# FoX queries, z and both merge gates in seven block products, with the token sums kept to the end

## The chip, the cores and the metric

The kernel runs on one core of one Trainium2 chip. The core has five engines with a queue each: TensorE (PE, matmuls into eight PSUM banks of 128 x 512 float32), VectorE (DVE), ScalarE (ACT), GpSimd (POOL) and SyncE (SP, which here only issues DMAs). Every engine works through its own queue in order and waits on semaphores for the others. The metric is the time of one execution in microseconds of device time. Before the change it was 949.82 us, the median of three runs (949.73 to 950.01).

## The reference

One layer of a hybrid decoder on 512 tokens, with 16 meta tokens ahead of them (L = 528), width 1024, in float32. A forgetting attention (FoX, 8 heads of 128) and an mLSTM (4 heads, keys of 256, values of 512) work on the same normalised input; sigmoid gates merge them, and an output projection and a norm follow.

```python
h = rms_norm(x, g_pre)
z = h @ w_in
(fq, fk, fv, ff, fz, mqk, mv, mi, mf, mo, mz, ga, gb) = jnp.split(z, SPLIT_POINTS, axis=-1)
oa = forgetting_attention(fq, fk, fv, log_sigmoid(ff + b_fox_f))      # softmax(scores + decay) v
ya = (oa * silu(fz)) @ w_a
hb = sigmoid(mo) * mlstm_scan(conv_silu(mq), conv_silu(mk), mv, mi, log_sigmoid(mf))
yb = (rms_norm(hb, g_head) * silu(mz)) @ w_b
merged = sigmoid(ga) * ya + sigmoid(gb) * yb
out = x + rms_norm(merged @ w_o, g_post)
```

## The kernel before

Float32 matmuls are made of three products of a two-part split: each operand is cut into a high part (an ACT copy to float32r) and a low part (a DVE subtraction), and `mm3` issues high x high, high x low, low x high (L149 to L151). The input is kept transposed as `hh` and `hl` (128 x 8 x 528), the sixteen meta tokens once more as the packed tile `hm`. Weights come by SP in raw tiles of 512 KB (`wload`, four buffers), and `wsplit` cuts them (ACT L141, DVE L143).

A projection of 256 columns is a *plain* unit: `proj_t` twice, 2 x 8 x 3 = 48 matmuls of 512 columns. The mLSTM's output gate `mo` and its z gate `mz` go by *seven block products* instead (Strassen's scheme in Winograd's form): `st_narrow` loads one half of the rows into r0 and the other into r1 and makes four splits, a (128 x 512, in the buffers `whs` and `wls`, two of each), b, c and d (128 x 1024); POOL adds two block sums into r0 between a and b (L259, L260), DVE two into r1 between c and d (L265, L266). `st_products` multiplies them with sums of token blocks (t1 to t4, made once by `st_tokens` and held in the pool `mlstm`), 84 matmuls of 256 columns in two PSUM banks; ACT takes three snapshots in passing (L313, L317, L321), and DVE combines the result in PSUM (L324, L325, L327).

The order in the program: the mLSTM head by head (h = 0 to 3: q and k with their convolution, values, output gate, then `value_part` of chunks 3 and 2, mz unit 0, chunks 1 and 0, mz unit 1; the transposes `pht` of the head's output follow in `turn_part`, the product with w_b into `yb` in `wb_part`). In `value_part` the sums of squares go to POOL for a power (`pow`, L797), and DVE multiplies the result into `ht` (L798); `pht` transposes `ht`. Then the pool `mlstm` is closed and `fox` is opened in its place. FoX goes by pairs of heads (p = 0 to 3): `fq_part`, `fk_part`, for even p `fv_part` of four heads, `prob_part` (logits `pl` on PE, a reduction on DVE with the decay row `ab`, exponential on ACT, `pn` on DVE and POOL), `ptr_part` (transposes `pt`, splits `pth` and `ptl`), `fz_part`, `fout_part`. The gate `gb` is applied to `yb` on POOL in odd p. At the end come `ga`, the product with w_a, the merge, and w_o.

Which instruction stands where in an engine's queue is set when the program is built: a scheduler orders the instructions of all engines by the order of the code and by its own estimates of when operands and buffers come free. Buffers of one tag come around in a ring: a tile waits until the tile before it in the same buffer has been read for the last time. The same holds for the eight PSUM banks.

## Time and profile before

| | |
|---|---|
| median of three runs | 949.82 us |
| profiled execution | 950.76 us |
| span of its instructions | 949.0 us |
| mean granted TensorE clock | 0.993 |
| busy PE, DVE, ACT, POOL | 930.5, 572.7, 440.0, 139.4 us |

Times in rows of the profile count from the start of the span. A row of the timeline gives start, duration, engine, line, operation, the tile written and the tiles read; in square brackets stands how long the engine had been idle before and what ended that. Names leave the buffer numbers out.

### The profile page before, as it was taken

The numbers are of one execution on the slowest core, as the hardware profiler recorded it, in microseconds if no ns is written. First come the engines' busy times: TensorE is split into PE (matmuls) and PEld (weight loads), VectorE is DVE, ScalarE is ACT, GpSimd is POOL, SyncE is SP. The second block draws the span as 40 slices with busy tenths as digits, with TensorE's granted clock in tenths as the row PEclk, the third lists the DMA queues.
The fourth block names the chain that finished last, engine by engine and source line by source line (L and its number), as shares of the span: only waits on it lengthen the run. The fifth ranks groups of instructions, "written<-read, shape, count | busy, mean of one in ns | idle before, by whom it ended". The sixth has DMA issues, their size and how long they took to land.

```text
span 949.0 us, 14296 instructions
## 1 busy us (share of the span) xinstructions
PE 930.5 (98%) x5720; PEld 835.3 (88%) x5720; DVE 572.7 (60%) x966; ACT 440.0 (46%) x740; POOL 139.4 (15%) x186
## 2 busy tenths in 40 slices
...
GB/s 227 92 62 87 45 112 87 121 27 90 98 103 100 59 75 90 112 78 89 54 100 173 89 129 79 96 96 118 89 96 95 90 71 85 177 89 95 105 23 90
DMA packets 71469, 90.05 MB, mean 95 GB/s; under 512 B 4965, under 2 KB 56261, under 8 KB 71402
## 3 DMA queue, kind: packets, MB, share of 16 engines
...
## 4 chain that ended last, share of the span: by engine, by line
PE 93%; DVE 4%; ACT 1%; issue 1%; DMA 0%; POOL 0%; DVEq 0%; POOLq 0%; ACTq 0%
PE pyb L150 3%; PE pyb L151 3%; PE pyb L149 3%; PE pv L151 3%; PE pv L149 3%; PE pv L150 3%; PE po L149 3%; PE po L150 3%; PE po L151 3%; PE pz L149 3%; PE pz L151 3%; PE pz L150 3%; PE pqk L149 2%; PE pqk L151 2%; PE pqk L150 2%; PE pfk L149 2%
## 5 line engine op out<-in xcount | busy, mean ns | idle before, releaser
L959 POOL TENSOR_SCALAR pn<-lt,rsum 128x128 f32<-128x128 f32 x32 | 23.2, 725 | 208.5 <-DVE rsum L957 208.5
L151 PE MATMUL pyb<-bh,wb_l 128*128 128x512 f32 x128 | 49.8, 389 | 0.0
L150 PE MATMUL pyb<-bl,wb_h 128*128 128x512 f32 x128 | 49.8, 389 | 0.0
L149 PE MATMUL pyb<-bh,wb_h 128*128 128x512 f32 x128 | 49.8, 389 | 0.0
L150 PE MATMUL pv<-wv_l,hh 128*128 128x512 f32 (+1 forms) x128 | 46.6, 364 | 1.5 <-DVE wv_l L143 1.5
L149 PE MATMUL pv<-wv_h,hh 128*128 128x512 f32 (+1 forms) x128 | 46.4, 362 | 0.0
L151 PE MATMUL pv<-wv_h,hl 128*128 128x512 f32 (+1 forms) x128 | 46.4, 362 | 0.0
L690 DVE SCALAR_TENSOR_TENSOR y<-z,gc,y 128x512 f32<-128x512 f32 (+1 forms) x48 | 35.9, 754 | 2.2 <-ACT y L683 1.5
L149 PE MATMUL pqk<-hh,wq_h 128*128 128x258 f32 x128 | 36.4, 284 | 0.0
L149 PE MATMUL pqk<-hh,wk_h 128*128 128x264 f32 x128 | 36.3, 284 | 0.0
L149 PE MATMUL pfk<-hh,wfk_h 128*128 128x264 f32 x128 | 36.3, 284 | 0.0
L151 PE MATMUL pfk<-hh,wfk_l 128*128 128x264 f32 x128 | 36.3, 284 | 0.0
L150 PE MATMUL pfk<-hl,wfk_h 128*128 128x264 f32 x128 | 36.3, 283 | 0.0
L151 PE MATMUL pqk<-hh,wk_l 128*128 128x264 f32 x128 | 36.3, 283 | 0.0
L150 PE MATMUL pqk<-hl,wk_h 128*128 128x264 f32 x128 | 36.2, 283 | 0.0
L151 PE MATMUL pqk<-hh,wq_l 128*128 128x258 f32 x128 | 36.0, 282 | 0.0
L150 PE MATMUL pqk<-hl,wq_h 128*128 128x258 f32 x128 | 36.0, 282 | 0.0
L150 PE MATMUL pout<-wo_l,mh 128*128 128x256 f32 (+1 forms) x96 | 30.6, 318 | 0.0
L151 PE MATMUL pout<-wo_h,ml 128*128 128x256 f32 (+1 forms) x96 | 30.6, 318 | 0.0
L149 PE MATMUL pout<-wo_h,mh 128*128 128x256 f32 (+1 forms) x96 | 30.6, 318 | 0.0
L956 ACT ACTIVATE lt<-lt,mn 128x144 f32<-128x144 f32 (+3 forms) x32 | 18.3, 573 | 24.7 <-DVE mn L951 24.7
L150 PEld LDWEIGHTS pv<-wv_l,hh 128*128 128x128 f32 x128 | 24.1, 189 | 5.5 <-DVE wv_l L143 1.7
...
## 6 DMA issues: line engine op xcount, KB each, us to landing
...
```

The costliest lines, as they stand in the source:

```text
L149: T.matmul(ps, ah, bh, start=start, stop=False, **kw)
L150: T.matmul(ps, ah, bl, start=False, stop=False, **kw)
L151: T.matmul(ps, al, bh, start=False, stop=stop, **kw)
L690: V.scalar_tensor_tensor(y[:, t0:L], z[:, m, t0 + j:L + j], gc[:, j * 16 + mi:j * 16 + mi + 1], y[:, t0:L], ALU.mult, ALU.add)
L956: S.activation(lt[:, 0:kn], lt[:, 0:kn], AF.Exp, bias=mn[:, li:li + 1], scale=-1.0, accum_out=rsum)
L959: G.tensor_scalar(pn[:, o:o + P].rearrange("p (g t) -> p g t", g=4), lt[:, 0:32].unsqueeze(1).to_broadcast([P, 4, 32]), rsum, None, ALU.mult)
```

## The change

Sixteen units change from plain to seven block products: `fq`, `fz`, `gb` and `ga`, four each, by a new helper `st_unit`, which `mz_part` uses as well. For this the token sums t1 to t4 must live to the end; their pool is renamed and never closed, and room is found for it: `whs` and `wls` have one buffer instead of two, the decay rows `ab` one instead of two, `hm` lies in the pad of `hh` (112 partitions in place of 128), the decay table `ac` is packed, the z gate is kept in `yb`, and FoX's output replaces it there. So `yb` times sigmoid(`gb`) goes to DRAM (`d_yb`, from POOL's queue), three of the four sigmoid(`ga`) too (`d_sa`, from ACT's queue), and both come back by SP in the last stage. The order of FoX is new: `ga` 0 and `gb` 0 are done beside the last w_b product, `gb` 1 and `gb` 3 at the end of even p, `gb` 2 and `ga` 1 in odd p, `ga` 2 and `ga` 3 at the end; the four products with w_a then follow each other.

```diff
-BYTES = {"w": 8192, "y": 2304, "vm": 2560, "ptm": 2048, "ab0": 5632, "ab1": 5632, "whs": 2048, "wls": 2048,
-         **{f"qk{i}{x}": 4608 for i in range(2) for x in "hl"}, **{f"v{x}": 8704 for x in "hl"},
-         **{f"big_{x}": 8704 for x in "hl"}}
+BYTES = {"w": 8192, "y": 2304, "vm": 2560, "ptm": 2048, "sg": 4160, "ab": 5632, "whs": 2048, "wls": 2048,
+         **{f"qk1{x}": 4608 for x in "hl"}, **{f"v{x}": 8704 for x in "hl"}, **{f"big_{x}": 8192 for x in "hl"}}
...
+    hhm = cp.tile([P, KC, LP], F32R, name="hh")
+    hh, hm = hhm[:, :, 0:L], hhm[:, :, L:LP]
...
-    c1 = ctx.enter_context(ExitStack())
-    mw = c1.enter_context(tc.tile_pool(name="mlstm", bufs=1))
+    mw = ctx.enter_context(tc.tile_pool(name="sums", bufs=1))
...
-        o = {"a11": split(r0[:, :, a], f"{name}a", ("whs", "wls"), mw, 2)}
+        o = {"a11": split(r0[:, :, a], f"{name}a", ("whs", "wls"), mw, 1)}
         G.tensor_tensor(r0[:, :, a], r0[:, :, a], r0[:, :, b], ALU.add)
         G.tensor_tensor(r0[:, :, b], r0[:, :, b], r1[:, :, b], ALU.add)
...
+    def st_unit(c0, name, room):
+        ps = banks(f"p{name}", 2)
+        st_products(st_narrow(c0, f"w{name}"), [(ps[0], ps[1], room.rearrange("p a (b n) -> p (a b) n", b=2), None)])
+        return ps
     def mz_part(h, u):
         g = sb([P, 2, SEQ], F32, ("qk1h", "qk1l")[u], f"gz{h}{u}")
-        ps = banks(f"pz{h}{u}", 2)
-        snap = g.rearrange("p a (b n) -> p (a b) n", b=2)
-        st_products(st_narrow(C_MZ + h * MV + u * 256, f"wz{h}{u}"), [(ps[0], ps[1], snap, None)])
+        ps = st_unit(C_MZ + h * MV + u * 256, f"z{h}{u}", g)
         for m in range(2):
             S.activation(g[:, m, :], ps[m], AF.Sigmoid)
         for m in range(2):
...
-        w = wchunk(win, 0, KC, C_FQ + p * 256, 256, f"wfq{p}")
-        ps = banks(f"pfq{p}", 2)
-        for m in range(2):
-            proj_t(ps[m], w, m)
+        ps = st_unit(C_FQ + p * 256, f"fq{p}", sb([P, 2, SEQ], F32, "w", f"fqs{p}"))
         s = -(FD ** -0.5)
...
     def fz_part(p):
-        w = wchunk(win, 0, KC, C_FZ + p * 256, 256, f"wfz{p}")
-        ps = banks(f"pfz{p}", 2)
-        for m in range(2):
-            proj_t(ps[m], w, m)
-        sz = sb([P, 2, SEQ], F32, "sz", f"fsz{p}", gp)
+        sz = yb[:, 2 * p:2 * p + 2, :]
+        ps = st_unit(C_FZ + p * 256, f"fz{p}", sz)
         for m in range(2):
             S.activation(sz[:, m, :], ps[m], AF.Sigmoid)
             V.tensor_tensor(sz[:, m, :], ps[m], sz[:, m, :], ALU.mult)
-        return sz
-    def gb_part(u):
-        w = wchunk(win, 0, KC, C_GB + u * 256, 256, f"wgb{u}")
-        ps = banks(f"pgb{u}", 2)
-        for m in range(2):
-            proj_t(ps[m], w, m)
-        sg = sb([P, 2, SEQ], F32, "sgb", f"sgb{u}", gp)
+    def gate_part(c0, u, name):
+        sg = sb([P, 2, SEQ], F32, "sg", f"s{name}{u}", gp)
+        ps = st_unit(c0 + u * 256, f"{name}{u}", sg)
         for m in range(2):
             S.activation(sg[:, m, :], ps[m], AF.Sigmoid)
-        G.tensor_tensor(yb[:, 2 * u:2 * u + 2, :], yb[:, 2 * u:2 * u + 2, :], sg, ALU.mult)
+        return sg
+    def gb_part(u):
+        sg = gate_part(C_GB, u, "gb")
+        y = yb[:, 2 * u:2 * u + 2, :]
+        G.tensor_tensor(y, y, sg, ALU.mult)
+        nc.gpsimd.dma_start(d_yb[u], y)
+    def ga_part(u):
+        nc.scalar.dma_start(d_sa[u], gate_part(C_GA, u, "ga"))
 
     def prob_part(p, m, q, k):
 
         h = 2 * p + m
         qh, ql = q
         kh, kl = k
-        ab = sb([P, NA], F32, ("ab0", "ab1")[m], f"ab{h}", gp)
+        ab = sb([P, NA], F32, "ab", f"ab{h}", gp)
         nc.sync.dma_start(ab, d_na[h:h + 1, :].to_broadcast([P, NA]))
         pn = sb([P, NPACK], F32, "w", f"pn{h}")
...
+        V.tensor_tensor(yb[:, h, :], ps, yb[:, h, :], ALU.mult)
...
+    gp = ctx.enter_context(tc.tile_pool(name="fox", bufs=1))
+    d_yb = [dram.tile([P, 2, SEQ], F32, name=f"d_yb{u}") for u in range(4)]
+    d_sa = [dram.tile([P, 2, SEQ], F32, name=f"d_sa{u}") for u in range(3)]
     q = fq_part(0)
-    c1.close()
-    gp = ctx.enter_context(tc.tile_pool(name="fox", bufs=1))
-    oss = line(gp, "oss", NCH * 3).rearrange("p (b i) -> p b i", i=3)
-    go = gp.tile([P, FH, SEQ], F32, tag="go", name="go")
     k = fk_part(0)
+    ga_part(0)
     wb_part(MH - 1, bt)
+    gb_part(0)
     for p in range(FH // 2):
         if p:
             q = fq_part(p)
-            fout_part(*tail)
+            if p % 2 == 0:
+                fout_part(*tail)
             k = fk_part(p)
         pn0 = prob_part(p, 0, q, k)
         if p % 2 == 0:
             v = fv_part(p)
-            pt0 = ptr_part(p, 0, pn0)
-            pn1 = prob_part(p, 1, q, k)
-            sz = fz_part(p)
-            fout_part(p, 0, pt0, v, sz)
-            pt1 = ptr_part(p, 1, pn1)
         else:
-            sz = fz_part(p)
-            pt0 = ptr_part(p, 0, pn0)
-            pn1 = prob_part(p, 1, q, k)
-            gb_part(p - 1)
-            fout_part(p, 0, pt0, v, sz)
-            pt1 = ptr_part(p, 1, pn1)
-            gb_part(p)
-        tail = (p, 1, pt1, v, sz)
+            fz_part(p)
+        pt0 = ptr_part(p, 0, pn0)
+        pn1 = prob_part(p, 1, q, k)
+        if p % 2 == 0:
+            fz_part(p)
+        elif p == 1:
+            gb_part(2)
+        else:
+            ga_part(1)
+        fout_part(p, 0, pt0, v)
+        pt1 = ptr_part(p, 1, pn1)
+        tail = (p, 1, pt1, v)
+        if p % 2 == 0:
+            gb_part(p + 1)
+            fout_part(*tail)
+    ga_part(2)
+    gs = [gsplit(p, (sb([P, 2, SEQ], F32R, f"qk{p}h", f"gh{p}"), sb([P, 2, SEQ], F32R, f"qk{p}l", f"gl{p}")))
+          for p in range(2)]
+    gs.append(gsplit(2, pair("w", "g2")))
     fout_part(*tail)
-    gs0 = gsplit(0, ("vh", "vl"))
-    sa2 = sb([P, 2, 2, SEQ], F32, "w", "sa")
-    sa0 = ga_part(0, sa2)
...
+    def fetch(tag, name, src):
+        t = sb([P, 2, SEQ], F32, tag, name, mw)
+        nc.sync.dma_start(t, src)
+        return t
     mh_, ml_ = [], []
-    for u, (t, pool) in enumerate((("qk0{}", wk), ("qk1{}", wk), ("ab{}", gp), ("s{}", gp))):
-        th, tl = (t.format(x) for x in (("01", "01", "01", ("z", "gb"))[u] if u > 1 else "hl"))
-        mh_.append(sb([P, 2, SEQ], F32R, th, f"mh{u}", pool))
-        ml_.append(sb([P, 2, SEQ], F32R, tl, f"ml{u}", pool))
-    gs = (gs0, gs1)
+    xr = []
     for u in range(4):
-        sa = sa0 if u == 0 else sa1 if u == 1 else ga_part(u, sa2)
         w2 = wchunk(wa, 0, KC, u * 256, 256, f"wa{u}")
+        sa = fetch(("t3h", "t1h", "t4h")[u], f"sa{u}", d_sa[u]) if u < 3 else sa3
+        sb_ = fetch(("t3l", "t1l", "t4l", "t2h")[u], f"sy{u}", d_yb[u])
         py = banks(f"pya{u}", 2)
         for m in range(2):
             for k in range(KC):
-                gh, gl = gs[k // 4]
+                gh, gl = gs[k // 2]
                 mm3(py[m], w2[0](k, m * P, m * P + P), w2[1](k, m * P, m * P + P),
-                    gh[:, k % 4, :], gl[:, k % 4, :], k == 0, k == KC - 1)
+                    gh[:, k % 2, :], gl[:, k % 2, :], k == 0, k == KC - 1)
         for m in range(2):
             V.tensor_tensor(sa[:, m, :], py[m], sa[:, m, :], ALU.mult)
-        V.tensor_tensor(sa, sa, yb[:, 2 * u:2 * u + 2, :], ALU.add)
-        S.activation(mh_[u], sa, AF.Copy)
-        V.tensor_tensor(ml_[u], sa, f(mh_[u]), ALU.subtract)
+        V.tensor_tensor(sa, sa, sb_, ALU.add)
+        if u < 3:
+            mh, ml = pair(("vl", "big_h", "big_l")[u], f"m{u}")
+        else:
+            mh, ml = sb([P, 2, SEQ], F32R, "ab", "mh3", gp), sb([P, 2, SEQ], F32R, "t2l", "ml3", mw)
+        S.activation(mh, sa, AF.Copy)
+        V.tensor_tensor(ml, sa, f(mh), ALU.subtract)
+        mh_.append(mh)
+        ml_.append(ml)
+        if u < 2:
+            for i in range(2):
+                b = 2 * u + i
+                xr.append(sb([P, DM], F32, (("t3h", "t3l"), ("t1h", "t1l"))[u][i], f"xr{b}", mw))
+                nc.sync.dma_start(xr[b], x2[b * P:(b + 1) * P, :])
```

Three places in the queues (from L187 on, lines of the changed kernel lie up to 19 further on than before: L798 is L806 there, and the multiply L919 is L921). First DVE in mLSTM head 1, from the last sum of squares to the combining of mz unit 0 (`pz_0`, `pz_1`); `wz11a` to `wz11d` are the weight splits of mz unit 1. Before:

```order
L795 TENSOR_SCALAR mss_2541<-mss_2541 128x1
L798 TENSOR_SCALAR ht_2502<-ht_2502,mrs_2544 128x512
L251 TENSOR_TENSOR wz11c_l<-wz_r_2726,wz11c_h 128x1024
L265 TENSOR_TENSOR wz_r_2726<-wz_r_2724,wz_r_2726 128x4x128
L266 TENSOR_TENSOR wz_r_2726<-wz_r_2726 128x4x128
L251 TENSOR_TENSOR wz11d_l<-wz_r_2726,wz11d_h 128x1024
L324 TENSOR_TENSOR pz_1_2549<-gz_2547,pz_1_2549 128x256
L327 TENSOR_TENSOR pz_0_2548<-pz_0_2548,gz_2547 128x512
```

Now:

```order
L803 TENSOR_SCALAR mss_2540<-mss_2540 128x1
L806 TENSOR_SCALAR ht_2501<-ht_2501,mrs_2543 128x512
L251 TENSOR_TENSOR wz11a_l<-wz_r_2723,wz11a_h 128x512
L251 TENSOR_TENSOR wz11b_l<-wz_r_2723,wz11b_h 128x1024
L251 TENSOR_TENSOR wz11c_l<-wz_r_2725,wz11c_h 128x1024
L265 TENSOR_TENSOR wz_r_2725<-wz_r_2723,wz_r_2725 128x4x128
L266 TENSOR_TENSOR wz_r_2725<-wz_r_2725 128x4x128
L251 TENSOR_TENSOR wz11d_l<-wz_r_2725,wz11d_h 128x1024
L324 TENSOR_TENSOR pz_1_2548<-gz_2546,pz_1_2548 128x256
L327 TENSOR_TENSOR pz_0_2547<-pz_0_2547,gz_2546 128x512
```

The narrow split a and split b of unit 1, which were made during the output gate (a stands ahead of `wz10c`, b among the first row sums, further up), now stand between the last multiply into `ht` and split c.

On POOL at the same place the two adds of unit 1 (L259, L260 on `wz_r_2724` before, on `wz_r_2723` now) and the powers. Before:

```order
L259 TENSOR_TENSOR wz_r_2550<-wz_r_2550 128x4x128
L260 TENSOR_TENSOR wz_r_2550<-wz_r_2550,wz_r_2552 128x4x128
L259 TENSOR_TENSOR wz_r_2724<-wz_r_2724 128x4x128
L260 TENSOR_TENSOR wz_r_2724<-wz_r_2724,wz_r_2726 128x4x128
L797 TENSOR_TENSOR mrs_2509<-mss_2506,mhalf 128x1
L797 TENSOR_TENSOR mrs_2544<-mss_2541,mhalf 128x1
```

Now:

```order
L259 TENSOR_TENSOR wz_r_2549<-wz_r_2549 128x4x128
L260 TENSOR_TENSOR wz_r_2549<-wz_r_2549,wz_r_2551 128x4x128
L805 TENSOR_TENSOR mrs_2508<-mss_2505,mhalf 128x1
L805 TENSOR_TENSOR mrs_2543<-mss_2540,mhalf 128x1
L259 TENSOR_TENSOR wz_r_2723<-wz_r_2723 128x4x128
L260 TENSOR_TENSOR wz_r_2723<-wz_r_2723,wz_r_2725 128x4x128
```

The adds have moved behind the two powers of the chunks 3 and 2.

Then DVE in FoX with p = 0, from split b of gate unit 1 on, while PE is in FZ (`pfz` are the two banks of the z gate, `wgb1` the weights of gate unit 1, which PE turns to after `fout` and `pt`). Now:

```order
L251 TENSOR_TENSOR wgb1b_l<-wgb_r_6589,wgb1b_h 128x1024
L965 RECIPROCAL rsum_6414<-rsum_6414 128x1
L969 TENSOR_SCALAR pn_6361<-lt_6402,rsum_6414 128x512
L251 TENSOR_TENSOR wgb1c_l<-wgb_r_6591,wgb1c_h 128x1024
L265 TENSOR_TENSOR wgb_r_6591<-wgb_r_6589,wgb_r_6591 128x4x128
L266 TENSOR_TENSOR wgb_r_6591<-wgb_r_6591 128x4x128
L324 TENSOR_TENSOR pfz_1_6420<-yb,pfz_1_6420 128x256
L325 TENSOR_TENSOR pfz_1_6420<-pfz_1_6420,yb 128x512
L327 TENSOR_TENSOR pfz_0_6419<-pfz_0_6419,yb 128x512
L251 TENSOR_TENSOR wgb1d_l<-wgb_r_6591,wgb1d_h 128x1024
L921 TENSOR_TENSOR yb<-pfz_0_6419,yb 128x512
```

Before, two plain splits of `wfk` stood here among the multiplies that empty `pfz`; now the splits a (further up), b and c of the next block unit and its two adds stand ahead of the combining, and the multiplies (L921) stand behind split d.

More of the change, by code (lines that the diff above doesn't have):

```diff
@@ L185, in proj_wide @@
                 for k in (k0, k0 + 1):
[L186 to L187 removed]
+                    T.matmul(pm[0:MP], hm[:, k, :], w[0](k, 0, 512), start=(k == 0), stop=False)
+                    T.matmul(pm[0:MP], hm[:, k, :], w[1](k, 0, 512), start=False, stop=(k == KC - 1))
     def proj_m(ps, w, n=256):
         for k in range(KC):
[L192 to L193 removed]
+            T.matmul(ps[0:MP], hm[:, k, :], w[0](k, 0, n), start=(k == 0), stop=False)
+            T.matmul(ps[0:MP], hm[:, k, :], w[1](k, 0, n), start=False, stop=(k == KC - 1))
     def v_meta(vm, ps):
[L197 removed]
+        S.activation(vm[0:MP], ps[0:MP], AF.Copy)
         V.tensor_tensor(vm[32:64, :], ps[32:64, :], f(vm[32:64, :]), ALU.subtract)
@@ L418, in v_tiles @@
         G.memset(f(vh[:, :, MV:MV + 2]), 1.0)
[L419 removed]
+        G.memset(f(vm[0:MP, MV:MV + 2]), 0.0)
         G.memset(f(vm[0:32, MV:MV + 2]), 1.0)
[L421 removed]
+        G.memset(f(vm[96:MP, MV:MV + 2]), 1.0)
         return vh, vl, vm
@@ L574, in tile_hybrid_block @@
     for i in range(2):
-        T.transpose(pm2[0:12, i * P:i * P + P], gn[:, NCH, i * 12:i * 12 + 12], ident)
+        T.transpose(pm2[0:12, i * P:i * P + MP], gn[0:MP, NCH, i * 12:i * 12 + 12], ident[0:MP, 0:MP])
     pst = psum1("gct")
@@ L603, in tile_hybrid_block, with acc @@
     V.tensor_tensor(a, gi, bc, ALU.subtract)
-    ac = sb([12, NCH, L], F32, "big_h", "ac")
+    ac = sb([12, NA], F32, "big_h", "ac")
+    def acc(c, k0, k1, rows=12):
+        return ac[0:rows, OFFA[c] + k0:OFFA[c] + k1]
     for c in range(NCH):
         k0, k1 = NM + c * P, NM + (c + 1) * P
-        V.tensor_scalar(ac[:, c, 0:k0], ac[:, c - 1, 0:k0] if c else a[:, 0:k0], bc[:, k0 - 1:k0], None, ALU.add)
-        V.tensor_copy(ac[:, c, k0:k1], a[:, k0:k1])
+        V.tensor_scalar(acc(c, 0, k0), acc(c - 1, 0, k0) if c else a[:, 0:k0], bc[:, k0 - 1:k0], None, ALU.add)
+        V.tensor_copy(acc(c, k0, k1), a[:, k0:k1])
     mp = line(cp, "mp", NCH, 12)
@@ L629, in tile_hybrid_block @@
         k1 = NM + (c + 1) * P
-        G.tensor_scalar(na[:, OFFA[c]:OFFA[c] + k1], ac[0:8, c, 0:k1], -1.0, None, ALU.mult)
+        G.tensor_scalar(na[:, OFFA[c]:OFFA[c] + k1], acc(c, 0, k1, 8), -1.0, None, ALU.mult)
     nc.sync.dma_start(d_na, na)
@@ L636, in columns @@
         for i, (c, j) in enumerate(BLK):
-            T.transpose(pcv[:, i, :], ac[:, c, NM + j * P:NM + (j + 1) * P], ident[0:12, 0:12])
+            T.transpose(pcv[:, i, :], acc(c, NM + j * P, NM + (j + 1) * P), ident[0:12, 0:12])
         for c in range(NCH):
```

63 lines of the change are left out of this document (24 added, 39 removed).

## The prediction

> **What bounds the kernel now.** I read the page first (busy time, slices, chain), then the waits of PE, then the times at which stages start on PE.
>
> ```profile
> span 949.0 us, 14296 instructions
> PE 930.5 (98%) x5720; PEld 835.3 (88%) x5720; DVE 572.7 (60%) x966; ACT 440.0 (46%) x740; POOL 139.4 (15%) x186
> DMA packets 71469, 90.05 MB, mean 95 GB/s; under 512 B 4965, under 2 KB 56261, under 8 KB 71402
> ...
> PE 93%; DVE 4%; ACT 1%; issue 1%; DMA 0%; POOL 0%; DVEq 0%; POOLq 0%; ACTq 0%
> ```
>
> PE is busy 98% of the span and 93% of the chain that ended last, so the kernel lasts as long as its matmuls are issued without a gap. In PE's waits, what stands behind the first 110 us is only this:
>
> ```profile
> PE pl L149 <- DVE fvm L198: 1.3, 2, 0.6
> PE pl L149 <- DVE fsz L919: 1.1, 2, 0.5
> ```
>
> Four waits, 2.4 us in all. So two questions decide the change: how much matmul time it takes away, and whether DVE, ACT and POOL, which get more to do, still deliver before PE arrives. Their average share (60%, 46%, 15%) does not answer the second.
>
> **The gain on PE.** Stage lengths, from the first matmul of a stage to the first of the next:
>
> ```profile
> 810.78 0.39 PE L149 MATMUL pga<-hh,wga_h 128*128 128x512 f32 x1
> ...
> 832.57 0.39 PE L149 MATMUL pya<-gh,wa_h 128*128 128x512 f32 x1
> ```
>
> ```profile
> 488.12 0.28 PE L149 MATMUL pz<-hh,wz30a_h 128*128 128x256 f32 x1
> ...
> 497.85 0.28 PE L777 MATMUL pnb<-vh,wh 128*128 128x258 f32 x1
> ```
>
> Two plain units (96 matmuls of 512 columns) last 21.79 us, 10.90 each. A unit of seven block products (84 of 256 columns) lasts 9.73. Sixteen units change: FQ, FZ, GB, GA, four each. 16 x (10.90 - 9.73) = **18.7 us**. The four waits above disappear too, since the order around them is a new one: 2.4 us. Gain without any new wait: 21.1 us.
>
> **What it adds.** Each unit gains, beside the splits of its weights, a narrow split, two adds on POOL (L259, L260), two adds on DVE (L265, L266), three snapshots on ACT and three combining operations on DVE. None of it is on PE; it costs something only where PE must wait. Two things make this likely, and I follow each by the rows.
>
> *mLSTM, head by head.* One buffer in place of two for the narrow split (whs, wls): the second mz unit of a head can make its narrow split only when PE has used that of the first unit. In the changed order it stands behind both ht multiplies, and POOL's two adds stand behind the pow operations, where before both were done during the output gate. Head 1 now:
>
> ```profile
> 225.11 1.41 POOL L260 TENSOR_TENSOR wz_r<-wz_r,wz_r 128x512 f32<-128x512 f32 x1 [13.26 <-DMA wz_r<-in_w_in_dram]
> 229.56 1.29 POOL L259 TENSOR_TENSOR wz_r<-wz_r 128x512 f32<-128x512 f32 x1 [3.03 <-DVE wz11a_l L251]
> 230.93 2.15 POOL L260 TENSOR_TENSOR wz_r<-wz_r,wz_r 128x512 f32<-128x512 f32 x1
> ...
> 243.72 0.49 DVE L798 TENSOR_SCALAR ht<-ht,mrs 128x512 f32<-128x512 f32 x1 [0.66 <-POOL mrs L797]
> 244.84 1.23 DVE L251 TENSOR_TENSOR wz11c_l<-wz_r,wz11c_h 128x1024 fp32r<-128x1024 f32 x1 [0.63 <-ACT wz11c_h L249]
> 246.10 0.69 DVE L265 TENSOR_TENSOR wz_r<-wz_r,wz_r 128x512 f32<-128x512 f32 x1
> ...
> 248.70 1.23 DVE L251 TENSOR_TENSOR wz11d_l<-wz_r,wz11d_h 128x1024 fp32r<-128x1024 f32 x1 [1.19 <-ACT wz11d_h L249]
> 249.84 0.42 DVE L324 TENSOR_TENSOR pz<-gz,pz 128x256 f32<-128x256 f32 x1
> ...
> 251.37 0.21 DVE L783 TENSOR_SCALAR r<-pnb,col 128x1 f32<-128x1 f32 x1
> ...
> 259.54 0.49 DVE L798 TENSOR_SCALAR ht<-ht,mrs 128x512 f32<-128x512 f32 x1 [0.66 <-POOL mrs L797]
> ...
> 261.69 0.27 PE L808 MATMUL pht<-ident,ht 128*128 128x128 f32 x1
> ```
>
> ```profile
> 243.75 1.06 ACT L249 ACTIVATE wz11c_h<-wz_r 128x1024 fp32r<-128x1024 f32 x1 [0.39 <-PE pz L150]
> ```
>
> The new chain, from the end of the ht multiply at 244.2: narrow split 0.69 (244.9), POOL's adds 1.29 and 1.41, the short rows because DVE is idle then (247.6), the ACT half of split b 1.06 and of c 1.06 (249.7), DVE's halves of b and c 1.23 each (251.1), two adds 0.69 each (252.5), ACT's half of d 1.06 (253.6). So wz11d_l starts at 253.6, not at 248.70: 4.9 us late; with the 2.15 row 5.6. Queued behind it on DVE stand the combining of the first unit, the row sums r and the last two ht multiplies. The final one ended at 260.03, 1.66 before PE turned to pht (261.69). 4.9 - 1.66 gives a wait of 3.2, with 5.6 3.9: I take 3.4 for heads 1 and 2. Head 0 has the combining ahead of split d: 3.4 less one split, 2.2. In head 3 the adds of wfq0 also stand ahead of the pow operations on POOL: 3.8. Sum **12.8 us**. From both sides: 0 if the slack in that queue is larger than I see, 4 x 3.9 = 15.6 by the long rows.
>
> *FoX, around each FZ unit.* The unit that follows FZ takes the PSUM bank of pfz_0, which comes free with the multiply of L919 (L921 in the changed kernel). That multiply, and the combining before it, now stand behind the splits a, b, c and both adds of the unit that follows. Before, FZ with plain products looked so:
>
> ```profile
> 588.20 0.39 PE L149 MATMUL pfz<-hh,wfz_h 128*128 128x512 f32 x1
> ...
> 599.12 0.39 PE L993 MATMUL pfo<-pth,fvh 128*128 128x512 f32 x1
> ...
> 601.26 0.27 PE L974 MATMUL pt<-ident,pn 128*128 128x128 f32 x1
> ...
> 602.71 0.48 PE L149 MATMUL pfq<-hh,wfq_h 128*128 128x512 f32 x1
> ```
>
> ```profile
> 589.24 0.31 DVE L951 CUSTOM_DVE_ANT_0 lt<-pl,ab 128x144 f32<-128x144 f32 x1
> ...
> 591.81 0.35 DVE L961 TENSOR_SCALAR pn<-lt,rsum 128x256 f32<-128x256 f32 x1
> ...
> 594.92 0.49 DVE L961 TENSOR_SCALAR pn<-lt,rsum 128x512 f32<-128x512 f32 x1
> 596.63 0.69 DVE L919 TENSOR_TENSOR fsz<-pfz,fsz 128x512 f32<-128x512 f32 x1 [1.22 <-ACT fsz L918]
> ```
>
> ```profile
> 594.70 1.28 ACT L918 ACT_TABLE_LOAD   x1
> 596.00 0.60 ACT L918 ACTIVATE fsz<-pfz 128x512 f32<-128x512 f32 x1
> ```
>
> ```profile
> 593.28 0.60 POOL L959 TENSOR_SCALAR pn<-lt,rsum 128x128 f32<-128x128 f32 x1 [0.65 <-DVE rsum L957]
> ```
>
> Zero is PE's start on fz (588.20 there). The second pn ended 4.0 us after it (592.16); no wfq_l split stands ahead of the chain now, by my estimate 0.5 earlier: 3.5. Narrow split 0.69 (4.2). POOL's first add 1.29 (5.5), the pn that follows it in POOL's queue 0.60 (6.1), the second add 1.9, between its short and long row, since DVE works beside it (8.0). ACT's half of b 1.06 (9.1), DVE's 1.23 (10.3), the last pn with its reciprocal 0.7 (11.0), DVE's half of c (12.2), two adds (13.6), three combining operations 1.5 (249.84 to 251.37; 15.1), table load 1.28 and sigmoid 0.60 beside split d (17.0), multiply 0.69 (17.7). PE is ready for the next unit after fz 9.73 and 3.59 of fout and ptr (599.12 to 602.71): 13.3. Wait 4.4; if the table is loaded during the combining 3.7. I take 4.1, for GB 1 and GB 3: 8.2. For odd p the following unit is GB 2 or GA 1. PE has ptr (601.26 to 602.71, 1.45) and the logits in between:
>
> ```profile
> 627.45 0.23 PE L149 MATMUL pl<-fkh,fqh 128*128 128x144 f32 x1
> ...
> 629.45 0.40 PE L149 MATMUL pfz<-hh,wfz_h 128*128 128x512 f32 x1
> ```
>
> 9.73 + 1.45 + 2.00 = 13.2. Ahead of the multiply stand, beside the combining at 15.1, two ptl, split d and two reductions, in whose 2.3 us table load and sigmoid are done: 17.4, a wait of 4.2 each, 8.4. After GB 2, FQ 2 takes the bank of a fout whose multiply stands behind the rest of the probabilities and the first two splits of wfq2, by the same kind of adding 3.4 more; GA 2 about 1 (estimates). Sum **21.0 us**; bounds 0 and 25, the latter with the long POOL row everywhere.
>
> The rest I cost at nothing. The one ab buffer is loaded again during a whole FZ or FV stage, and its masks are added there. The first of these loads now stands on SP ahead of a wo load and the write of d_nm, some 30 us before PE needs them. The stores of yb and sigmoid(ga), 3.5 MB out and 3.5 back, are some 75 us of traffic at the mean of 95 GB/s, spread over 400. In the tail a wa unit has 10.9 us of PE against four additions and multiplications and two splits on DVE, some 6.3 us. If that last cover fails it costs some 2.
>
> **Sum.** 950.76 (the profiled execution: span 949.0 and 1.76 around it) - 21.1 + 12.8 + 21.0 = 963.5. The median of the runs shown was 949.82, 0.94 lower: **962.5**.
>
> **Rivals.**
> (1) *The waits stay hidden in FoX.* The four block units per head that exist already end their work in time: for mz 1.66 us are left at pht. If the FoX chain is as short as that of mz, all 21.0 go and only the mLSTM waits stay: 949.8 - 21.1 + 12.8 = 941.5; if those go as well, 928.7. For it speaks that PE waits on these units nowhere now; against it, that each mz unit has its adds done before PE arrives, which in FoX the order does not allow. Faster in any case.
> (2) *The clock falls after each wait.* Around 102 us PE waited for yb:
>
> ```profile
> PE ps L149 <- ACT yb L737: 3.2, 1, 3.2
> ```
>
> ```profile
> 100.00:105.00 5.00, 2.15 (x7) 1.28 (x8) 2.51 (x3) 4.72 (x7) 0.00 (x0) 0.81 0.37 112
> 105.00:110.00 5.00, 3.95 (x15) 3.27 (x16) 4.12 (x10) 1.66 (x4) 0.00 (x0) 0.50 0.01 2
> 110.00:114.00 4.00, 4.00 (x23) 4.00 (x23) 1.84 (x6) 0.72 (x2) 0.10 (x1) 0.58 0.00 0
> 114.00:118.00 4.00, 4.00 (x36) 4.00 (x36) 2.21 (x9) 0.72 (x2) 1.10 (x2) 1.00 0.00 0
> ```
>
> The number third from the end is the granted clock, the x in the first bracket the matmuls: 0.50 after the wait of 3.2 us, and 23 matmuls in 4 us in place of 36. With PE busy throughout, 13/36 x 4 = 1.4 us were lost in 110 to 114 alone, perhaps 3 in all. The waits forecast are of 3 to 5 us; if eight of them each cost 3 more, the time is 962.5 + 24 = 986.5. Against it: that wait came with three shorter ones right behind it, those forecast stand between unbroken stages. The Trainium skill, page "TensorE: Matmul & The Clock Gate", section "What's actually happening", has the same rule: half clock after an idle window of about 3.4 us. The 0.50 here agrees; by that rule some of these waits would pay and some not, which is a chance and no sum.
> (3) *Gain and waits cancel.* If six tenths of both sums remain (33.8 x 0.6 = 20.3), because the queues hold more slack than I count everywhere: 949.8 - 21.1 + 20.3 = 949.0.
>
> **Numbers.** Forecast 0.48, with an own range of 951 to 978; (1) with its partial forms 0.32; (2) 0.14; (3) within 0.2% 0.06. A measurement tells 0.2% (1.9 us) from no change. Faster takes (1), 0.32; same 0.06; slower the forecast and (2), 0.62. The range holds 8 in 10 from 935, in the upper part of (1), to 987, the price of (2).
>
> **What would show it.** PE should wait at pht for DVE ht in each head (2 to 4 us), and at the first matmul of GB 1, GB 2, GB 3 and GA 1 for DVE L921 (4 to 5 us); the sixteen units should each last about 9.8 us less their waits. Wrong it would be if pht starts 9.8 us after the second mz unit, if the first matmuls of pgb follow without a gap, or if the clock row shows 0.5 behind those waits. The Trainium skill, page "GPSIMD Engine Reference", section "Specifications", says POOL shares its SBUF interface with VectorE; the rows 1.41 and 2.15 of one and the same add fit that, and longer adds there would show as larger waits.

## The result: slower by 0.9%, and the profile after

The changed kernel takes 958.09 us (median of four runs, 957.86 to 959.08) against 949.86 before: ratio 1.0089, 95% interval 1.0071 to 1.0106. The forecast was 962.5, slower, within 935 to 987. The profiled execution took 958.12 us. Its page, span, busy time and the shares of the chain that ended last:

```profile
span 956.3 us, 15752 instructions
PE 915.8 (96%) x6296; PEld 844.5 (88%) x6296; DVE 649.0 (68%) x1080; ACT 473.9 (50%) x818; POOL 194.1 (20%) x222
...
PE 73%; DVE 11%; issue 5%; POOL 5%; ACT 4%; DMA 1%; POOLq 0%; DVEq 0%; ACTq 0%
```

PE is busy 14.7 us less than before (930.5), and yet the span is 7.3 us longer: the matmul time was saved, and more than that came back as waiting. DVE and POOL, 4% and nothing of the chain before, are now 11% and 5% of it. Where the time lies is read from the starts of stages on PE. Before, the first q and k product of head 1, the first FoX query and the first product with w_o start here:

```profile
139.08 0.36 PE L149 MATMUL pqk<-hh,wq_h 128*128 128x258 f32 x1
...
511.97 0.47 PE L149 MATMUL pfq<-hh,wfq_h 128*128 128x512 f32 x1
...
897.85 0.39 PE L149 MATMUL pout<-wo_h,mh 128*128 128x512 f32 x1
```

And after the change:

```profile
136.55 0.36 PE L149 MATMUL pqk<-hh,wq_h 128*128 128x258 f32 x1
...
516.77 0.36 PE L149 MATMUL pfq<-hh,wfq0a_h 128*128 128x256 f32 x1
...
904.67 0.39 PE L149 MATMUL pout<-wo_h,m 128*128 128x512 f32 x1
```

Up to head 1 2.5 us are won; heads 1 to 3 take 380.22 in place of 372.89, 7.3 more; FoX up to w_o takes 387.90 in place of 385.88, 2.0 more, although it holds all of the gain of 21.1; the rest 0.5 more. Sum 7.3. PE's waits of the changed kernel (what it waited for, us in total, times, longest):

```profile
PE pfz L149 <- ACT yb L317: 6.7, 4, 2.2
PE pga L149 <- ACT sga L317: 3.6, 2, 2.0
PE pz L149 <- ACT gz L317: 3.5, 7, 0.8
PE pgb L149 <- DVE yb L921: 3.5, 2, 1.8
PE ps L149 <- ACT yb L741: 3.2, 1, 3.2
...
PE pl L149 <- DVE ptl L987: 2.0, 2, 1.0
PE pgb L149 <- ACT sgb L317: 1.6, 1, 1.6
...
PE pht L816 <- DVE ht L806: 1.2, 2, 0.6
PE pl L149 <- DVE mn L959: 1.0, 2, 0.5
```

The waits at `pht` and at L921 are there, but fewer and shorter than forecast: at `pht` two of 0.6 us in place of one of 2 to 4 in each head, at L921 1.74 and 1.75 before GB 1 and GB 3 in place of four of 4 to 5, and none before GB 2 and GA 1. The largest is a place which the forecast did not name: L317, the second snapshot that ACT takes *inside* a block unit, before PE may start the unit's last product (15.4 us in all). How it comes about shows in head 1 (the timeline of after: start, duration, engine, line, what is written and read, and the idle time before it with its releaser):

```profile
237.08 0.28 PE L149 MATMUL pz<-hh,wz10a_h 128*128 128x256 f32 x1
239.97 0.49 DVE L806 TENSOR_SCALAR ht<-ht,mrs 128x512 f32<-128x512 f32 x1 [0.66 <-POOL mrs L805]
241.14 1.29 POOL L259 TENSOR_TENSOR wz_r<-wz_r 128x512 f32<-128x512 f32 x1 [1.20 <-DVE wz11a_l L251]
242.50 1.28 POOL L260 TENSOR_TENSOR wz_r<-wz_r,wz_r 128x512 f32<-128x512 f32 x1
243.82 1.06 ACT L249 ACTIVATE wz11b_h<-wz_r 128x1024 fp32r<-128x1024 f32 x1 [3.15 <-POOL wz_r L260]
245.74 0.36 ACT L317 ACTIVATE gz<-pz 128x256 f32<-128x256 f32 x1
246.15 0.39 PE L149 MATMUL pz<-hh,wz10d_h 128*128 128x256 f32 x1 [0.59 <-ACT gz L317]
249.91 1.23 DVE L251 TENSOR_TENSOR wz11d_l<-wz_r,wz11d_h 128x1024 fp32r<-128x1024 f32 x1 [1.19 <-ACT wz11d_h L249]
...
261.34 0.30 PE L816 MATMUL pht<-ident,ht 128*128 128x128 f32 x1 [0.62 <-DVE ht L806]
```

ACT works through its queue in order. The snapshot of unit 0 stands there behind the split b of unit 1, and that split waits 3.15 us for POOL's second add. So PE, in the middle of unit 0, waits for a weight split of unit 1. In FoX, p = 0, the same on a larger scale:

```profile
613.13 0.28 PE L149 MATMUL pfz<-hh,wfz0a_h 128*128 128x256 f32 x1
...
614.42 0.28 PE L151 MATMUL pfz<-hh,wfz0a_l 128*128 128x256 f32 x1
614.88 0.61 ACT L249 ACTIVATE wgb1a_h<-wgb_r 128x512 fp32r<-128x512 f32 x1
...
617.50 1.29 POOL L259 TENSOR_TENSOR wgb_r<-wgb_r 128x512 f32<-128x512 f32 x1
618.77 0.71 POOL L967 TENSOR_SCALAR pn<-lt,rsum 128x128 f32<-128x128 f32 x1
619.45 1.28 POOL L260 TENSOR_TENSOR wgb_r<-wgb_r,wgb_r 128x512 f32<-128x512 f32 x1
620.76 1.06 ACT L249 ACTIVATE wgb1b_h<-wgb_r 128x1024 fp32r<-128x1024 f32 x1 [3.45 <-POOL wgb_r L260]
623.39 0.36 ACT L317 ACTIVATE yb<-pfz 128x256 f32<-128x256 f32 x1
623.81 0.39 PE L149 MATMUL pfz<-hh,wfz0d_h 128*128 128x256 f32 x1 [2.21 <-ACT yb L317]
...
630.08 1.29 DVE L921 TENSOR_TENSOR yb<-pfz,yb 128x512 f32<-128x512 f32 x2 [0.88 <-ACT yb L920]
630.92 0.36 PE L149 MATMUL pgb<-hh,wgb1a_h 128*128 128x256 f32 x1 [1.74 <-DVE yb L921]
```

GB 1 starts 17.79 us after FZ; the forecast's chain ended at 17.7. One chain, but PE meets it twice: 2.21 us inside FZ, at the snapshot, and 1.74 at the bank. The chain begins with the narrow split of GB 1 (`wgb1a`), which starts just after the last matmul that reads FZ's narrow split (`wfz0a`, 614.42): with one buffer it could not start earlier, so the single narrow buffer stands at the head of the chain in FoX as well.

### The profile page after: what moved, and what is told of

The parts are those of the page before. It is cut to its first block, busy times and chain, and to the rows that moved or that the text cites. A ratio compares the mean times of both kernels' runs of the same rounds, so it can differ in the third digit from the quotient of the medians.

```text
span 956.3 us, 15752 instructions
## 1 busy us (share of the span) xinstructions
PE 915.8 (96%) x6296; PEld 844.5 (88%) x6296; DVE 649.0 (68%) x1080; ACT 473.9 (50%) x818; POOL 194.1 (20%) x222
## 4 chain that ended last, share of the span: by engine, by line
PE 73%; DVE 11%; issue 5%; POOL 5%; ACT 4%; DMA 1%; POOLq 0%; DVEq 0%; ACTq 0%
PE pyb L150 3%; PE pyb L151 3%; PE pyb L149 3%; PE pv L151 3%; PE pv L150 3%; PE pv L149 3%; PE po L149 3%; PE po L151 3%; PE po L150 3%; PE pqk L149 3%; PE pqk L151 3%; PE pqk L150 3%; PE pfk L149 2%; PE pfk L151 2%; PE pfk L150 2%
## 5 line engine op out<-in xcount | busy, mean ns | idle before, releaser
L967 POOL TENSOR_SCALAR pn<-lt,rsum 128x128 f32<-128x128 f32 x32 | 31.1, 972 | 108.6 <-DVE rsum L965 58.6
L151 PEld LDWEIGHTS pyb<-bh,wb_l 128*128 128x128 f32 x128 | 24.0, 188 | 5.0
L149 PEld LDWEIGHTS pyb<-bh,wb_h 128*128 128x128 f32 x128 | 24.0, 188 | 4.9
L150 PEld LDWEIGHTS pyb<-bl,wb_h 128*128 128x128 f32 x128 | 24.0, 188 | 4.9
L149 PEld LDWEIGHTS pv<-wv_h,hh 128*128 128x128 f32 x128 | 24.2, 189 | 3.9
```

The lines of the kernel that those rows point to most:

```text
L149: T.matmul(ps, ah, bh, start=start, stop=False, **kw)
L150: T.matmul(ps, ah, bl, start=False, stop=False, **kw)
L151: T.matmul(ps, al, bh, start=False, stop=stop, **kw)
L967: G.tensor_scalar(pn[:, o:o + P].rearrange("p (g t) -> p g t", g=4), lt[:, 0:32].unsqueeze(1).to_broadcast([P, 4, 32]), rsum, None, ALU.mult)
```

## Experiments

The starts of three stages on PE and the span, read from the one profiled execution of each kernel, and the medians of all its executions. Most profiled executions lie within 1 us of the median; that of FZ plain (952.61) is 1.9 us above it, that of the shared bank (960.89) 1.8 below.

| kernel | head 1 | FoX | w_o | span | median |
|---|---|---|---|---|---|
| before | 139.08 | 511.97 | 897.85 | 949.0 | 949.86 |
| changed | 136.55 | 516.77 | 904.67 | 956.3 | 958.09 |
| before, one narrow buffer | 135.23 | 514.49 | 900.37 | 951.5 | 953.20 |
| changed, two in the mLSTM | 138.89 | 513.71 | 900.73 | 952.0 | 952.80 |
| changed, FZ plain | 137.00 | 517.23 | 899.31 | 950.5 | 950.74 |
| changed, adds on DVE | 133.07 | 505.92 | 888.15 | 939.4 | 941.06 |
| changed, second add on DVE | 134.82 | 509.77 | 892.64 | 943.9 | 945.65 |
| before, adds on DVE | 133.89 | 506.78 | 892.67 | 944.1 | 945.86 |
| changed, shared bank | 135.96 | 516.24 | 907.39 | 959.0 | 962.71 |
| changed, adds on DVE, shared bank | 134.37 | 507.21 | 883.55 | 934.8 | 936.44 |
| changed, stores twice | 136.44 | 516.73 | 908.99 | 960.5 | 961.56 |
| changed, no stores | 136.15 | 516.34 | 907.39 | 959.0 | 960.50 |

The kernel before, run beside them, had medians of 949.84, 950.02 and 950.12.

### One narrow buffer in the kernel before

```diff
-        o = {"a11": split(r0[:, :, a], f"{name}a", ("whs", "wls"), mw, 2)}
+        o = {"a11": split(r0[:, :, a], f"{name}a", ("whs", "wls"), mw, 1)}
```

> The kernel before with one thing taken from the change: one buffer instead of two for the narrow split (whs, wls). Theory A (the single buffer delays the second mz unit of a head): the time from pqk of one head to pqk of the next grows as in the changed kernel, by 2.2, 2.2 and 3.0 us for heads 1 to 3, so some 957 us, with waits of PE at pz for ACT gz and at pht for DVE ht. Rival B (the stretch in the mLSTM comes from something else that the change does there, the packed hm, the early ab load, the longer life of the sums): 950 us, no such waits.

953.20 us, ratio 1.0034 (1.0021 to 1.0046). PE's waits, of which the kernel before has neither:

```profile
PE pz L149 <- ACT gz L317: 2.5, 6, 0.6
PE pht L808 <- DVE ht L798: 1.9, 3, 0.7
```

Heads 1 to 3 take 379.26 us, 6.4 more than before: the single buffer alone makes most of the 7.3 that the change costs there, with the same two waits. But the time up to head 1 is 3.85 shorter, which was not expected: at 97 us DVE's add L266 of unit 0 ran beside POOL's L259 of unit 1 before, and took 1.66 us; with one buffer that add on POOL comes later, L266 takes 0.69, the narrow split of unit 1 (0.69) no longer stands ahead of it on DVE, and what follows on ACT up to the sigmoid comes 1.4 earlier:

```profile
PE ps L149 <- ACT yb L737: 1.7, 1, 1.7
```

That wait was 3.2. Most of the rest of the 3.85 is the granted clock, which stays at 1.00 behind this wait and was 0.50 before. The forecast had +2.2 in this place.

### Two narrow buffers again, in the mLSTM only

```diff
+    c1 = ctx.enter_context(ExitStack())
+    m2 = c1.enter_context(tc.tile_pool(name="narrow2", bufs=1))
...
-        o = {"a11": split(r0[:, :, a], f"{name}a", ("whs", "wls"), mw, 1)}
+        o = {"a11": split(r0[:, :, a], f"{name}a", ("whs", "wls"), pool, 1)}
...
-        ps = st_unit(C_MZ + h * MV + u * 256, f"z{h}{u}", g)
+        ps = st_unit(C_MZ + h * MV + u * 256, f"z{h}{u}", g, (mw, m2)[u])
...
     q = fq_part(0)
+    c1.close()
```

> The changed kernel with a second buffer for the narrow split as long as the mLSTM lasts (a pool of 4 KB that is closed before the FoX pool is opened). Theory A: the 7.3 us that heads 1 to 3 gained go, 958.1 - 7.3 = 950.8 us. Rival B: 958 us.

952.80, ratio to before 1.0031 (1.0018 to 1.0045). Heads 1 and 2 are back at 124.3 us each, the time before the change; head 1 starts at 138.89, near the old 139.08. Only head 3 keeps a wait of its own:

```profile
PE pht L818 <- DVE ht L808: 1.8, 1, 1.8
```

There the first FoX query's splits stand in the queues, as the forecast's larger figure for head 3 had it. So the buffer explains the mLSTM's share from both sides: taken away in the old kernel it costs 6.4, given back in the new one it returns heads 1 and 2 entirely. FoX takes 387.02 us, still 1.1 more than before with all of its gain in it; there the narrow buffer is still single. What a second one would be worth in FoX, where the narrow splits of GB 1 and GB 2 too start only when PE has used that of the unit before, no run tested.

### FZ plain

```diff
-        ps = st_unit(C_FZ + p * 256, f"fz{p}", sz)
+        w = wchunk(win, 0, KC, C_FZ + p * 256, 256, f"wfz{p}")
+        ps = banks(f"pfz{p}", 2)
+        for m in range(2):
+            proj_t(ps[m], w, m)
```

> The changed kernel with the four FZ units as plain products again (48 matmuls of 512 columns). Theory A (the waits around FZ come from its snapshots and its combining standing behind the splits of the unit that follows): the waits inside pfz (6.7 us), at pgb for the L921 multiply (3.5) and at pl behind FZ (3.0) go, some 13 us with the stretches beside them, against 4 x 1.17 = 4.7 us more of matmuls: 950 us. Rival B (the waits come from the load on DVE, ACT and POOL as a whole, and the next unit's splits are late anyway): the waits move to the unit that follows, 957 to 963 us.

950.74, ratio to before 1.0010 (1.0000 to 1.0019). The four FZ units have 4 x 1.17 = 4.7 us more matmul time than as block products, and the kernel is 7.3 faster than the changed one: as block products these four lose some 12. The waits at `pfz` and at L921 are gone. In FoX two of size remain: 1.9 us at GA 0's snapshot, and 3.3 before GA 2, where two gate units follow each other and the sigmoid of GA 1 stands on ACT behind two splits of GA 2.

### Both adds on DVE

```diff
-        G.tensor_tensor(r0[:, :, a], r0[:, :, a], r0[:, :, b], ALU.add)
-        G.tensor_tensor(r0[:, :, b], r0[:, :, b], r1[:, :, b], ALU.add)
+        V.tensor_tensor(r0[:, :, a], r0[:, :, a], r0[:, :, b], ALU.add)
+        V.tensor_tensor(r0[:, :, b], r0[:, :, b], r1[:, :, b], ALU.add)
```

> The changed kernel with the two adds between split a and split b on DVE (0.69 us each) instead of POOL (1.29 and 1.28, behind pn and pow). Theory A (the chain through POOL's adds is what makes split b, and so the snapshots behind it, late): split b starts some 1.3 us earlier everywhere, and some twelve waits of PE get shorter by up to that: 945 to 951 us. Rival B (DVE is what is full: 649 us busy, and 24 units x 1.4 us come to it): 958 us or more, up to 965.

941.06, ratio to before 0.9902 (0.9886 to 0.9918): the same change is now a gain. The add takes half the time on DVE, and it no longer waits behind `pn` and the powers. One group of this kernel, to be held against 1.28 and 1.29 above:

```profile
L260 DVE TENSOR_TENSOR wz_r<-wz_r,wz_r 128x512 f32<-128x512 f32 x8 | 5.5, 689 | 0.2
```

The heads take 124.3 us each although the narrow buffer is still single, and no wait for L317 is left. In FoX two FQ units still wait, 2.3 us (for L313, the first snapshot, in FQ 0) and 1.2; the largest is the wait at the bank, now in one piece:

```profile
PE pgb L149 <- DVE yb L921: 5.3, 2, 2.6
```

And behind it stands what rival (2) foretold. Stretches around its first one, which ends at 618.58 (third from the end the granted clock, in the first bracket PE's matmuls):

```profile
615.00:620.00 5.00, 2.36 (x16) 2.16 (x15) 4.14 (x8) 4.80 (x9) 0.27 (x1) 0.79 0.66 206
620.00:625.00 5.00, 5.00 (x26) 5.00 (x26) 3.99 (x7) 1.56 (x4) 0.00 (x0) 0.52 0.00 0
625.00:630.00 5.00, 5.00 (x46) 5.00 (x45) 2.45 (x2) 1.95 (x3) 0.00 (x0) 1.00 0.00 0
```

26 matmuls in 5 us in place of 46: GB 1 lasts 12.66 us and not 9.79, so the wait of 2.64 costs 2.87 more.

### The second add alone on DVE

```diff
-        G.tensor_tensor(r0[:, :, b], r0[:, :, b], r1[:, :, b], ALU.add)
+        V.tensor_tensor(r0[:, :, b], r0[:, :, b], r1[:, :, b], ALU.add)
```

> The changed kernel with only the second add (L260) on DVE, the first (L259) on POOL: tells which part of the way over POOL makes the wait. Theory A (what costs is that the second add stands behind pn or a power in POOL's queue and that split b waits for it): the snapshots L317 come about 1.3 + 0.7 us earlier, their waits of 1 to 2.2 us go nearly all, and most of the 17 us that both adds on DVE won are had: 940 to 946. Theory B (each hand-over between DVE and POOL costs, and one is left, from the narrow split to L259 and back to L260 on DVE, which now also holds up DVE's own queue while it waits): less than half is had, 950 to 957.

945.65, ratio to before 0.9946 (0.9930 to 0.9962), in the span of theory A. 12.4 of the 17.0 us are had with the add that split b waits for.

```profile
PE pgb L149 <- DVE yb L921: 4.0, 2, 2.0
...
PE pfz L149 <- ACT yb L317: 2.0, 2, 1.0
```

The snapshot waits at `pfz` fall from 6.7 to 2.0; so the second add's way over POOL is the larger part, and that of the first the smaller. How much of it is the place in POOL's queue and how much the length of the add (1.28 us there, 0.69 on DVE) this run does not separate.

### The same edit in the kernel before

Both adds on DVE, as above, without the change.

> The kernel before the change with both adds (L259, L260) on DVE instead of POOL: tells whether the 17 us that the changed kernel won by this edit (958.1 to 941.1) belong to the change's own chain or would be had without it. Theory A (the chain is the change's): before waits for none of these adds behind 110 us, so only its first 140 us can gain, where the wait of 3.2 us at ps and the clock of 0.50 behind it stand; at most the 6.0 us by which the second head starts earlier in the changed kernel with this edit (133.07 against 139.08), and nothing behind it: 944 to 949.9. Theory F (DVE's adds are faster wherever they stand, so that the edit is worth about the same in both kernels): 933 to 938. Should it be 944, the change is worth 941 - 944 = -3 us once the adds are on DVE.

945.86, ratio 0.9954 (0.9938 to 0.9971): theory A. All of the gain lies before head 1 (5.2 us); every later stage keeps its length (heads 124.28 to 124.33, FoX 385.89). In the front the edit moved ACT's order too. The table load of the sigmoid that PE waits for at `ps` stood behind split d before, at 99.92 us; with the adds on DVE it stands ahead of it, at 93.98, and the wait is gone.

With the adds on DVE in both, the change is worth 941.06 - 945.86 = -4.8 us; with them on POOL, +8.2. Of the 17.0 us that the edit wins in the changed kernel, some 13 are the change's own waits: heads 1 to 3 get 7.4 shorter there and FoX 5.7, and in the kernel before neither does.

### The bank shared instead

The four transposes `pt` of a head take a PSUM bank each; here those of chunks 0 and 2 share one, so that GB 1 and GB 3 need not take the bank of FZ.

```diff
-            pt = psum1(f"pt{h}{c}")
+            if c in (0, 1, 3):
+                bank = psum1(f"pt{h}{c}")
+            else:
+                bank = bank0
+            if c == 0:
+                bank0 = bank
+            pt = bank[:, 128:512] if c == 2 else bank
```

> The changed kernel in which the transposes of chunk 0 and chunk 2 of a head share one PSUM bank (128 and 384 columns), so that GB 1 and GB 3 need not take the banks of FZ. POOL keeps its adds. Theory A (two separate causes: the bank for the waits at pgb, the queue of ACT behind POOL's adds for the waits inside pfz): the waits at pgb for L921 (3.5 us) and the stretch of the transposes before it go, the waits of 6.7 us inside pfz stay: 951 to 955 us. Rival D (the wait inside pfz and that at pgb are one delay, and what is not waited for at pgb is waited for at the next split of wgb): 957 us or more.

962.71, ratio 1.0139 (1.0119 to 1.0159): slower than the changed kernel. The wait at L921 is gone, and a new one came in its place, with the snapshots still there (the `pfz` wait was 6.7):

```profile
PE pt L988 <- DVE ptl L993: 10.0, 8, 1.8
PE pfz L149 <- ACT yb L317: 5.7, 4, 1.7
```

The transposes of chunk 2 must wait until DVE has read the bank, in each of the eight heads, so the edit brings waits of its own. Around FZ 0 it shows that the bank was only the place where the delay was met: GB 1 starts 14.96 us after FZ in place of 17.79, but PE leaves it for the second head's transposes and waits 1.84 there, and GB 1 ends 27.19 after FZ's start in place of 27.60.

### Adds on DVE and the bank shared

Both edits above together, on the changed kernel.

> The kernel with the adds on DVE and, besides, one PSUM bank for the transposes of chunks 0 and 2. In the kernel with the adds on DVE alone PE waited 2.6 us at pgb 1 and pgb 3 for the L921 multiply, and the granted clock fell to 0.5 behind it. Theory A: both waits and both stretches at half clock go, 941 - 5.2 - 4.4 = 931 to 933 us. Rival D (the delay comes back at the next split): 937 to 941 us.

936.44, ratio to before 0.9854 (0.9839 to 0.9869), between the two expectations: the best version here, 13.4 us below the kernel before, and 9.4 below that kernel with its adds on DVE. With the adds out of POOL the wait at the bank goes for good; the transposes' own waits stay, and so does FQ 0's wait at its first snapshot:

```profile
PE pt L988 <- DVE ptl L993: 7.5, 8, 1.6
PE pfq L149 <- ACT fqs L313: 2.2, 1, 2.2
```

FoX takes 376.34 us, 9.5 less than before. Of the 18.7 + 2.4 of the forecast's gain that is a little under half.

### The stores twice, and not at all

Each store of yb and sigmoid(ga) is made once more, to a second place:

```diff
         nc.gpsimd.dma_start(d_yb[u], y)
+        nc.gpsimd.dma_start(d_y2[u], y)
...
-        nc.scalar.dma_start(d_sa[u], gate_part(C_GA, u, "ga"))
+        g = gate_part(C_GA, u, "ga")
+        nc.scalar.dma_start(d_s2[u], g)
+        nc.scalar.dma_start(d_sa[u], g)
```

> The changed kernel in which every store of yb and of sigmoid(ga) to DRAM is made twice (a second copy that nobody reads, 3.5 MB more of writes). Theory A (the way through DRAM is hidden): 958 us, within 1. Rival C (the stores hold up POOL's and ACT's queues, or the loads that share the DMA engines): each of the seven stores costs again what it costs now, 960 us or more.

961.56, ratio to before 1.0120 (1.0105 to 1.0135), 3.5 more than the changed kernel. Taken alone that would say the stores cost something. The opposite edit leaves them out:

```diff
-        nc.gpsimd.dma_start(d_yb[u], y)
...
-        nc.scalar.dma_start(d_sa[u], gate_part(C_GA, u, "ga"))
+        gate_part(C_GA, u, "ga")
...
+    d_yb = [x2[u * P:(u + 1) * P, :].rearrange("t (a n) -> t a n", a=2) for u in range(4)]
+    d_sa = d_yb
```

> The changed kernel without the seven stores to DRAM; what the last stage loads in their place is the input x, so the loads are all still made, and the merge is computed with other numbers. It tells what the stores (and the wait of the loads for them) cost. Theory A (as forecast, nothing): 957.2 to 959.1, like the changed kernel, unless the order of the work moves. Theory C (the stores cost as much as their doubling did, +3.5 us, in the tail above all): 953.5 to 955.5.

960.50, ratio 1.0109 (1.0094 to 1.0124): also slower than the changed kernel, by 2.4, which neither theory had. So more than the way over DRAM is measured by these two runs. Between the two profiled executions, 2.7 us apart, 1.34 arise in the product with w_b behind GA 0, where both kernels wait at the same snapshot. After the change that wait ends at 548.62 and is 1.97 long; the two stretches there:

```profile
548.00:552.00 4.00, 3.38 (x21) 3.05 (x22) 3.11 (x4) 2.85 (x5) 2.83 (x2) 1.00 0.08 27
552.00:556.00 4.00, 4.00 (x19) 3.34 (x18) 3.05 (x5) 1.09 (x2) 0.62 (x1) 1.00 0.64 153
```

Without the stores it ends at 548.34 and is 2.12 long:

```profile
548.00:552.00 4.00, 3.66 (x17) 3.28 (x18) 3.39 (x4) 2.57 (x5) 3.10 (x2) 0.69 0.01 2
552.00:556.00 4.00, 4.00 (x17) 3.25 (x16) 2.68 (x4) 1.09 (x2) 0.34 (x1) 0.88 0.67 181
```

The clock fell, and the product lasts 23.13 us in place of 21.79; another fall, to 0.83 from 833 to 843, stands behind GA 1's wait, and GA 2 starts 1.1 later after GA 1. With the stores twice the first place shows 0.71 and 0.86 behind a wait of 1.86, and the product lasts 23.13: 1.34 of the 4.2 us between the profiled executions. The rest there lies in the tail, where GA 2, GA 3 and the first w_a product come in another order and PE waits 2.1 for a split of w_a. A direct cost of the stores was not found, but with differences of 2 to 4 us from the clock and the order, one of 1 or 2 us would not be seen either; this stays open.

## Why the prediction was right, and where its terms were off

The direction, the size (962.5 against 958.1) and, in kind, the mechanism held: matmul time saved, and more given back where PE waits for DVE and ACT, which are behind with the splits of the following unit. The sum came out 5.4 us too high in the profiled execution (963.5 against 958.1). Its parts were further off than that and cancel in part, and most of the waiting lay at a place that was not forecast; so the nearness of the number is partly luck.

- **The gain, 18.7 + 2.4.** Held nearly. Undisturbed new units last 9.78 to 9.84 us in place of the 9.73 that was taken, some 1.2 us over sixteen; the plain ones had lasted 10.88 to 11.02, which gives 0.5 back; the four old waits did go.
- **FoX, waits of 21.0.** Measured 2.0 + 21.1 = 23.1 (the stretch took 2.0 us longer although 21.1 had been saved in it). By places: GB 1 and GB 3 4.1 forecast, 4.5 measured for GB 1 (17.79 less the 13.3 after which PE was to be ready: 2.21 in FZ, 1.74 at the bank, 0.5 in units that run a little longer). GB 2 and GA 1 4.2 forecast at the bank, where neither waited; 4.25 measured for GB 2 as 1.13 inside FZ, 1.5 at the logits and 1.62 inside GB 2. FQ 2, estimated at 3.4, waited 0.18, and GA 2 0.26 in place of 1; GA 0, for which nothing was forecast, waited 1.97. The remaining 3 us are in the same units, which lose a little beside each wait (FZ 0 lasts 12.22, 10.01 without its wait). So the length of the chain was right and the two estimates by likeness were not; that the sums agree, 21.0 and 23.1, is partly chance.
- **Where PE would wait.** The step that failed. The forecast followed the chain to the next unit's first matmul alone, and asked of ACT only when its splits are done. It did not ask what else stands in ACT's queue behind a split that waits for POOL: the running unit's snapshot. The waits at L317 make 15.4 us, those forecast at `pht` and L921 only 1.2 and 3.5. That L317 is the place and POOL's second add the larger cause, the two edits of the adds show: the waits at L317 fall to 3.1 with the second add on DVE and go with both.
- **The mLSTM, 12.8.** Too large in size, right in kind. Heads 1 to 3 cost 7.3 (10.6 forecast). The forecast let the chain start from the ht multiply as the old trace had it, ended 4.7 us after the start of unit 0 (239.51 to 244.2). In the new order that multiply ended at 240.46, 3.4 after the start (237.08), since the splits a and b of the second unit (0.69 and 1.21) no longer stand ahead of it on DVE, and two DVE operations that had run beside POOL's adds take 1.22 and 0.68 in place of 2.14 and 1.45. So split d began 12.8 us after the unit's start; 14.1 was forecast, and 9.2 was the old figure. A removed obstacle was counted as work that comes later, and not as room that opens earlier.
- **Head 0, 2.2 of it.** The stretch up to head 1 became 2.5 us shorter. The term itself is right in sign: from the first matmul of mz unit 0 to head 1 the changed kernel takes 24.49 us in place of 23.85, 0.6 more. But ahead of that it gains 3.2, most of it (2.2) in the 46 matmuls of the values ahead of that unit, 8.28 us in place of 10.44: the wait at `ps` is as long as before (3.2) but the clock did not fall after it. The kernel before with one buffer shows a second effect, a shorter wait (1.7), which the change itself does not have. Why the clock stayed up is not settled.
- **Costed at nothing.** The last part (0.5 longer) and the ab buffer gave no wait that could be named as theirs; the stores are open within 1 or 2 us.
- **The rivals.** (1) did not occur as stated, but its condition, a FoX chain as short as that of mz, can be made: with the adds on DVE the time is 941.06, by chance near the 941.5 that it named, and the mLSTM waits, not the FoX waits, are what went entirely. (2) did not occur in the profiled execution of the changed kernel (clock 0.999), whose waits in FoX came in pieces of at most 2.2 us; it did where the same chain was met in one piece of 2.6. That the length of the pieces is the reason is not shown: behind pieces of 1.86 to 2.2 us the clock fell in other kernels. (3) is refuted: 1.0071 is the lower end of the interval.
